# A two-layer trunk on one core: three plain items at the start of an up stage, residual rows scaled in the delta net's output projection, and five smaller edits beside them

## The chip, the cores and the metric

The kernel runs on one core of one Trainium2 chip. The metric is the device time of one execution in microseconds (us), the median of three runs. TensorE (PE in the profile) does the matrix products, VectorE (DVE) and ScalarE (ACT) the elementwise work, GpSimd (POOL) some of it, and SyncE (SP) issues most of the transfers between HBM and on-chip memory. Each engine works through its own instructions in a fixed order.

## The reference, cut to what matters

```python
e = jax.nn.silu(c @ cond_w + cond_b)
for i in range(2):                       # x is 1024 x 1024, f32
    sh1, sc1, g1, sh2, sc2, g2 = split(e @ ada_w[i] + ada_b[i], 6)
    y = mixers[i](x * (1 + sc1) + sh1)   # 0: gated delta net, 8 heads; 1: retention, 4 heads
    x = layer_norm(DN_ALPHA * x + (1 + g1) * y, ln_g[i, 0], ln_b[i, 0])
    y = conv_ffn(x * (1 + sc2) + sh2, ffn_up[i], ffn_conv_w[i], ffn_conv_b[i], ffn_down[i])
    x = layer_norm(DN_ALPHA * x + (1 + g2) * y, ln_g[i, 1], ln_b[i, 1])

def conv_ffn(h, w_up, conv_w, conv_b, w_down):      # hidden width 2816
    gate, up = split(h @ w_up, 2)
    gate = causal_dwconv(gate, conv_w) + conv_b     # 3 taps
    return (silu(gate) * up) @ w_down
```

The delta net projects h to q, k, v and a gate z, passes q, k and v through a causal convolution with 4 taps, solves one unit triangular system for every chunk of 64 positions, scans the chunks with a running state, and projects back. Retention projects to q, k, v and a gate, rotates q and k, and runs chunks of 128 positions with a running state.

## The kernel before, in words

Activations are kept transposed, as tiles of 128 features by 512 positions (a *half* is 512 of the 1024 positions). Nearly every product of two f32 matrices is made of three matmuls (`mm3`, lines 110 to 112, and line 637): each factor is split into a high part and a low rest, by one copy on ACT (line 89) and one subtraction on DVE (line 90). So before most matmuls stands a chain: a load by SP (`wr`), ACT, DVE, PE.

The stages follow one another: a short start that forms `e`; the delta net (`run` plans its order; on the profile's clock about 50 to 640 us); its output projection `proj_ln` in two halves (640 to about 770); up stage of the first feed-forward (about 750 to 1200); its down stage `proj_gen` (1200 to 1500); up stage of retention (about 1480 to 1780); retention's cores with `ret_fill` beside them (1780 to about 2150); output projection of retention; up stage (about 2290 to 2735) and down stage (to the end) of the second feed-forward.

**The delta net.** `run()` holds a clock of its own and takes the ready stream with the lowest number next; streams yield estimated times from the table `LAT`. `t_solve` (one call for four heads) does a forward substitution on DVE: 31 steps of two operations (lines 806 and 808), between a transpose into `Y` and two out, `RX` and `TX`. After every second step it yields `LAT["fs"]`, and other streams come in. `filler` is the stream of projection matmuls (tiles `acc<-hT,wl` and `acc<-hT,wh` in the views) that fill PE while DVE solves; each of its items also brings a convolution on DVE (line 456), a split, and at its end one `bg_step`. A `bg_step` does one unit of work left over from elsewhere: for `bg_ada` it is one load of 512 KB of `ada_w` (tile `mvw`) and two operations on DVE (lines 214 and 216), which form the modulation vectors of later stages as a matvec off PE. In this stage and in retention the load's tile has the tag `wr`, which the weight loads share; `bg_tag` names it.

**The up stages** are `strassen`. An *item* is a pair of weight blocks with a sink for its four outputs; two items, a gate and an up, make one of 11 pairs. All items but the first run as `wino`, which needs seven block products instead of eight, with DVE forming sums of weight blocks (`psub`, line 1205, `mm<-wr`) and of activations (`build_T`: tiles `T1` to `T4`). The first two items run plain, eight products each (tiles `acc<-hT,W`), while the activations are not ready: their first sides before `build_T` (kept in `ah`), the second sides behind it. `build_T` needs f32 values of the first half, which exist only as high and low parts, so PE adds the two with the identity (`joined`, line 402, `mm<-hT,ident_r`). `conv` (line 1579) is the gate's convolution. For retention (`direct`) the first sides go straight to their sinks; its sinks hold the rotations, and from item 8 on `scale_rows` has POOL multiply and add rows for the next residual (lines 1699 and 1700).

**The down stage** `proj_gen` reads its residual rows with `xload`; for the first half POOL scales them by `ln_g` and `ln_b` (line 1361). At the end of the kernel `norm` normalises the result's rows and stores them: the right half by ACT and POOL, the left by DVE (lines 1395 to 1403).

Of the kernel before, what the change touches and what calls it, by code (L numbers as in the profile page):

```python
# [11 lines left out]
AF = mybir.ActivationFunctionType  # L12
# [21 lines left out]
def trunk_kernel(ctx: ExitStack, tc, A):  # L34
# [82 lines left out]
    bg_tag = ["wr"]  # L117
# [83 lines left out]
    def bg_ada(i, j, kind):  # L201
        box = {}

        def unit(nh, kp):
# [3 lines left out]
            wr = tl(bg_tag[0], [P, 2, HALF], name="mvw")  # L208
            c0 = j * D + nh * HALF
            sp.dma_start(wr, A["ada_w"][i, kp * 256:(kp + 1) * 256, c0:c0 + HALF].rearrange("(a p) n -> p a n", p=P))  # L210
            for kk in range(2):
                k = kp * 2 + kk
                if k == 0:
                    dve.tensor_scalar(a, wr[:, 0], e[:, 0:1], None, ALU.mult)
                else:
                    dve.scalar_tensor_tensor(a, wr[:, kk], e[:, k:k + 1], a, ALU.mult, ALU.add)  # L216
# [157 lines left out]
    def ln_hooks(half, xts, tag, vecs2, out, dst, key, npool=0):  # L374
        def build(f):
            out.append(build_one(tag, xts, *vecs2(), f, pool if f < npool else dve))
        return ([lambda f=f: build(f) for f in range(KT)]
                + [lambda t=t: ln_store(half, t, xts, dst, key) for t in range(4)])

    def build_T(B, xts, scale, shift, tags, direct):  # L380
# [31 lines left out]
        def rest():  # L412
            if direct:
                for k in range(4):
                    t1, b22 = raw[k]
                    x11 = joined(B["11"][k])
                    dve.tensor_sub(b22, b22, t1)
                    put("T3", k, b22)
                    dve.tensor_add(b22, b22, x11)
                    put("T2", k, b22)  # L420
                    dve.tensor_sub(t1, t1, x11)
                    put("T1", k, t1)
                    dve.tensor_sub(b22, joined(B["21"][k]), b22)
                    put("T4", k, b22)
                return
            for k, (t1, b22) in enumerate(raw):
                dve.tensor_sub(t1, t1, joined(B["11"][k]))
                put("T1", k, t1)
            for k, (t1, b22) in enumerate(raw):
                dve.tensor_sub(b22, b22, t1)  # L430
                put("T2", k, b22)
            for k, (t1, b22) in enumerate(raw):
                dve.tensor_sub(t1, b22, joined(B["11"][k]))
                put("T3", k, t1)
            for k, (t1, b22) in enumerate(raw):
# [261 lines left out]
    def give(tag, n):  # L697
        free[tag] += n
# [88 lines left out]
    def t_solve(qd_):  # L787
        yield after_ev(("T0", 2 * qd_ - 1), ("A", 2 * qd_), ("A", 2 * qd_ + 1))
        yield from take("lane", 1)
        X = tl("lane", [P, 32, 32], name="X")  # L790
# [27 lines left out]
        give("lane", 1)  # L818
        emit(("Tq", qd_))
# [228 lines left out]

    def filler(items):
        spare = [(z, k) for k in range(GH)]  # L1050
        todo = list(items)
        while todo or spare:
# [39 lines left out]
            bg_step(acc_tile)  # L1092

    LAT = {"kk": 3.05, "ld": 1.14, "g1": 17.30, "gm": 2.50, "mm": 1.81, "T": 4.98, "X": 3.38, "fs": 1.9, "T0": 5.00, "t1": 1.65, "t2": 2.35, "t3": 1.34, "D": 2.67, "s1": 1.60, "s2": 1.22, "s3": 1.26, "tail": 12.31, "ssq": 9.30, "fv": 2.85}
# [58 lines left out]
    def strassen(hT0, xts, scale, shift, items, tags=("hTb", "hTb", "qkv", "qkv", "aux"), direct=False, beside=None, spare="lane"):  # L1153
# [19 lines left out]
        for n in range(2):  # L1173
# [6 lines left out]
            ahead.append([tl("cv", [P, 516], name="ah")[:, 0:HALF] for _ in range(2)])  # L1180
            for t, x in zip(ahead[n], X):
                act.activation(t, x, AF.Copy)
        rest = build_T(B, xts, scale, shift, tags, direct)
# [24 lines left out]
        def wino(n, sink):  # L1208
            ua, ub = items[n][:2]
            wa, wb = tl("wr", [P, D]), tl("wr", [P, D])  # L1210
            sp.dma_start(wa, ua)
            anchor["i"] = sp.dma_start(wb, ub)
            if beside:
                beside(n)
            a11, a12, a21, a22 = wa[:, hs(0)], wa[:, hs(1)], wb[:, hs(0)], wb[:, hs(1)]
# [26 lines left out]
        for n in range(2):  # L1242
# [11 lines left out]
        for n in range(2, len(items)):  # L1254
# [731 lines left out]
```

## Time and profile before

| | |
|---|---|
| median of the three runs | 2977.0 us (2974.75, 2977.0, 2977.12) |
| the profiled execution's own time | 2971.39 us |
| its span on the core | 2969.6 us |
| PE busy | 2819.0 us (95%) |
| DVE busy | 2214.7 us (75%) |
| ACT busy | 1323.3 us (45%) |
| POOL busy | 598.5 us (20%) |
| DMA, mean | 149 GB/s, 442.34 MB |

A time is read with its span: 1.8 us lie around the span. Busy shares are means over very unlike stages, so the views that matter are those of one stage or one stretch: the timeline of an engine with its idle times and what ended them, and the busy time by stretch.

### The profile page before, as it was taken

To read this page: it belongs to the slowest core of one execution; us is meant where nothing else is said; L and a number is where in the kernel's file an instruction comes from. 1 tells how busy PE (TensorE), PEld (TensorE's weight loads), DVE (VectorE), ACT (ScalarE), POOL (GpSimd) and SP (SyncE) were. 2 spreads that over 40 slices of the span, in tenths; PEclk is the share of its full clock that TensorE was granted. 3 is DMA by queue.
4 is the path that set the end of the run, shared out by engine and by line. 5 is a ranking of instruction groups with operands and counts; after the bars stand their busy time and mean duration, and the time that the engine had idled before them with its cause. 6 is when DMAs were issued, how large, how long until landed. Compare 5 with 4: busy or idle time off the path is not lost.

```text
span 2969.6 us, 38837 instructions
## 1 busy us (share of the span) xinstructions
PE 2819.0 (95%) x13654; PEld 2302.7 (78%) x13654; DVE 2214.7 (75%) x3863; ACT 1323.3 (45%) x2463; POOL 598.5 (20%) x625
## 2 busy tenths in 40 slices
PE   8889998999999999999999989999999899999997
PEld 7768877887778888777787777767778678888786
DVE  5795687546688888997677765666787787778889
ACT  4655555433444444536533332222345544445443
POOL 0411221134011111520002330322201011112603
PEclk9999999999999999999999999999999999999999
DMA  7222221344244444863424453556574243325753
GB/s 276 88 75 70 98 90 65 114 165 144 104 149 156 163 157 148 320 198 124 158 84 145 161 212 116 165 170 184 180 246 151 95 138 107 106 100 196 246 178 118
DMA packets 235378, 442.34 MB, mean 149 GB/s; under 512 B 22192, under 2 KB 75696, under 8 KB 235184
## 3 DMA queue, kind: packets, MB, share of 16 engines
q1 hardware_dynamic: 205024, 387.96, 38.7%
q10 hardware_dynamic: 25152, 34.61, 3.2%
q0 software_dynamic: 5008, 17.30, 1.5%
q8 instruction: 107, 1.75, 0.2%
q14 instruction: 87, 0.71, 0.1%
HBM read 331.26 MB, written 108.53 MB: 148 GB/s over the span
## 4 chain that ended last, share of the span: by engine, by line
PE 67%; DVE 15%; DMA 7%; issue 6%; ACT 3%; POOL 1%; SPq 0%; DVEq 0%; ACTq 0%; POOLq 0%
PE acc L637 15%; PE acc L1463 9%; PE acc L1159 8%; PE acc L110 5%; PE acc L111 5%; PE acc L112 5%; PE sc L1159 4%; PE sc L637 4%; PE sc L1463 2%; PE mm L637 2%; PE sc L110 2%; PE sc L111 2%; PE sc L112 2%; DMA mvw<-in_ada_w 1%; DVE qkv L456 1%
## 5 line engine op out<-in xcount | busy, mean ns | idle before, releaser
L1463 PE MATMUL acc<-bb,ab 128*128 128x512 f32 x1800 | 429.5, 393 | 5.3 <-DVE bb L90 3.6
L1463 PEld LDWEIGHTS acc<-bb,ab 128*128 128x128 f32 x1800 | 338.1, 189 | 79.9 <-DVE bb L90 5.9
L637 PE MATMUL acc<-hT,wh 128*128 128x512 f32 x960 | 301.1, 395 | 0.0
L1600 POOL TENSOR_TENSOR o<-o 128x512 f32<-128x512 f32 x88 | 118.4, 1356 | 725.3 <-DVE o L1593 690.3
L1159 PE MATMUL acc<-T,wb 128*128 128x512 f32 x840 | 204.8, 393 | 9.5 <-DVE wb L90 9.5
L637 PEld LDWEIGHTS acc<-hT,wh 128*128 128x128 f32 x960 | 183.3, 191 | 34.2
L637 PE MATMUL acc<-hT,wl 128*128 128x512 f32 x480 | 203.5, 424 | 0.2 <-ACT sg L1085 0.2
L89 ACT ACTIVATE ab<-ar 128x512 fp32r<-128x512 f32 x210 | 129.2, 624 | 149.7 <-PE acc L1463 75.0
L1159 PEld LDWEIGHTS acc<-T,wb 128*128 128x128 f32 x840 | 158.0, 189 | 46.6 <-DVE wb L90 13.8
L90 DVE TENSOR_TENSOR ab<-ar,ab 128x512 fp32r<-128x512 f32 x210 | 171.3, 822 | 28.3 <-ACT ab L89 28.0
L90 DVE TENSOR_TENSOR wb<-wr,wb 128x512 fp32r<-128x512 f32 x162 | 115.7, 719 | 88.7 <-ACT wb L89 86.8
L90 DVE TENSOR_TENSOR wl<-wr,wh 128x1024 fp32r<-128x1024 f32 x85 | 104.7, 1232 | 88.3 <-ACT wh L89 88.3
L89 ACT ACTIVATE wh<-wr 128x1024 fp32r<-128x1024 f32 x101 | 106.8, 1059 | 127.4 <-PE acc L637 62.2
L90 DVE TENSOR_TENSOR wb<-mm,wb 128x512 fp32r<-128x512 f32 x216 | 145.0, 684 | 20.4 <-ACT wb L89 18.5
L89 ACT ACTIVATE wb<-mm 128x512 fp32r<-128x512 f32 x216 | 122.4, 593 | 76.5 <-DVE mm L1205 76.2
L1218 ACT ACTIVATE pc<-acc 128x512 f32<-128x512 f32 x143 | 84.7, 592 | 158.6 <-PE acc L1159 106.5
L89 ACT ACTIVATE wb<-wr 128x512 fp32r<-128x512 f32 x162 | 99.2, 626 | 91.6 <-DMA wr<-in_ffn_up 48.8
L637 PE MATMUL acc<-wh,hT 128*128 128x512 f32 x384 | 136.9, 419 | 2.2 <-DVE vv L90 1.1
L1579 DVE SCALAR_TENSOR_TENSOR o<-g,vc,o 128x512 f32<-128x512 f32 (+2 forms) x176 | 135.1, 787 | 0.7
L456 DVE SCALAR_TENSOR_TENSOR qkv<-raw,vc,qkv 128x512 f32<-128x512 f32 x144 | 114.7, 800 | 28.0 <-ACT qkv L454 27.0
L110 PE MATMUL acc<-T,wb 128*128 128x512 f32 x292 | 116.4, 399 | 17.1 <-DVE wb L90 16.5
L216 DVE SCALAR_TENSOR_TENSOR ada<-mvw,e,ada 128x512 f32<-128x512 f32 x140 | 106.7, 762 | 25.1 <-DMA mvw<-in_ada_w 24.9
(636 smaller groups left out, 7056.8 us busy)
## 6 DMA issues: line engine op xcount, KB each, us to landing
wr<-in_ffn_up SPq DMA_DIRECT2D x96, 512.0 KB, 4.3
mvw<-in_ada_w SPq DMA_DIRECT2D x80, 512.0 KB, 4.2
ad<-o SPq DMA_DIRECT2D x154, 256.0 KB, 2.3
ar<-ad SPq DMA_DIRECT2D x154, 256.0 KB, 3.9
Br<-in_ffn_down SPq DMA_DIRECT2D x66, 256.0 KB, 3.7
wr<-in_ret_wv SPq DMA_DIRECT2D x32, 512.0 KB, 3.6
ar<-od SPq DMA_DIRECT2D x56, 256.0 KB, 4.8
xs<-xt ACTq DMA_DIRECT2D x24, 512.0 KB, 3.0
```

The source lines that it names most:

```text
L89: act.activation(dst_h, src, AF.Copy)
L90: eng.tensor_tensor(dst_l, src, dst_h, ALU.subtract)
L110: mm(acc, wl[:, k], hl[0], start=first, stop=False)
L111: mm(acc, wh[:, k], hl[1], start=False, stop=False)
L112: mm(acc, wh[:, k], hl[0], start=False, stop=last)
L216: dve.scalar_tensor_tensor(a, wr[:, kk], e[:, k:k + 1], a, ALU.mult, ALU.add)
L456: dve.scalar_tensor_tensor(oh, raw[:, 3 - j:515 - j], w[:, 3 - j:4 - j], oh, ALU.mult, ALU.add)
L637: pq(pe.matmul(out, lhsT, rhs, start=start, stop=stop, **kw), cost)
L1159: return pe.matmul(*a, skip_group_check=True, **kw)
L1463: mm_ = (lambda *a, p=p, onto=onto, **kw: (mm if p < 2 else pe.matmul)(*a, skip_group_check=onto, **kw))
L1579: dve.scalar_tensor_tensor(tv, gv[:, c0 - j:c1 - j], w[:, 2 - j:3 - j], tv, ALU.mult, ALU.add)
L1600: pool.tensor_tensor(o[d], o[x], o[y], op)
```

## The change

The edits, in the order of the program:

1. `bg_tag` is `"xT"` in the delta net and in retention: a load of `ada_w` goes, as two loads of 256 KB, into a ring of two tiles of its own; elsewhere it is as before.
2. `filler` counts the `bg_step` calls that it owes; while a `t_solve` runs it makes none, and behind it up to two per item. `LAT["fs"]` goes from 1.9 to 2.2.
3. The first half's rows of x behind the first layer norm are scaled by `ln_g` and `ln_b` on DVE before they are stored, in the hooks of `proj_ln`'s second half (`store_scaled`, 16 operations), and the down stage of the first feed-forward no longer scales them on POOL (16 fewer).
4. `build_T` has one order, that of retention, for all up stages: per k instead of per tile name, with 8 joins instead of 12.
5. The up stages of the feed-forwards run three items plain instead of two: 12 matmuls more in each (8 products of 12 instead of 7). The third item's first side waits in two `xT` tiles.
6. In retention's up stage every third raw weight block is loaded in two halves into `xT` tiles: a third buffer beside two of `wr`.
7. `scale_rows` comes with items 4 to 11 instead of 8 to 15.
8. `norm` at the end does both halves on DVE, with four operations of two steps.

```diff
-    bg_tag = ["wr"]
+    bg_tag = ["xT"]
...
+            if bg_tag[0] == "xT":
+                wr = [tl("xT", [P, HALF], name="mvw") for _ in range(2)]
+                for a2 in range(2):
+                    sp.dma_start(wr[a2], src[:, a2])
...
+    def store_scaled(t, xts, dst, key, grows):
+        for hf in range(2):
+            for r, op in zip(grows, (ALU.mult, ALU.add)):
+                dve.tensor_tensor(xts[t][:, hs(hf)], xts[t][:, hs(hf)], r[hf], op)
+        ln_store(0, t, xts, dst, key)
...
         def rest():
-            if direct:
-                for k in range(4):
...
-            for k, (t1, b22) in enumerate(raw):
-                dve.tensor_sub(t1, t1, joined(B["11"][k]))
-                put("T1", k, t1)
...
+            for k in range(4):
+                t1, b22 = raw[k]
+                x11 = joined(B["11"][k])
+                dve.tensor_sub(b22, b22, t1)
+                put("T3", k, b22)
+                dve.tensor_add(b22, b22, x11)
+                put("T2", k, b22)
+                dve.tensor_sub(t1, t1, x11)
+                put("T1", k, t1)
                 dve.tensor_sub(b22, joined(B["21"][k]), b22)
                 put("T4", k, b22)
...
     def t_solve(qd_):
...
+        busy.append(qd_)
...
+        busy.clear()
...
-            bg_step(acc_tile)
...
+            owed[0] += 1
+            for _ in range(0 if busy else min(owed[0], 2)):
+                bg_step(acc_tile)
+                owed[0] -= 1
...
-        for n in range(2):
+        nd = 2 if direct else 3
+        for n in range(nd):
             X = side(n, 0)
...
-            wa, wb = tl("wr", [P, D]), tl("wr", [P, D])
-            sp.dma_start(wa, ua)
-            anchor["i"] = sp.dma_start(wb, ub)
+            raws = []
+            for m, u in ((2 * n, ua), (2 * n + 1, ub)):
+                if direct and m % 3 == 0:
+                    raws += [tl("xT", [P, HALF], name="wr") for _ in range(2)]
+                    for h2 in range(2):
+                        anchor["i"] = sp.dma_start(raws[-2 + h2], u[:, hs(h2)])
...
-        for n in range(2, len(items)):
+        for n in range(nd, len(items)):
...
-            if half == 0 and gain:
+            if half == 0 and gain and not scaled:
                 for r, op in zip(grows, (ALU.mult, ALU.add)):
                     for hf in range(2):
                         pool.tensor_tensor(xt[:, hs(hf)], xt[:, hs(hf)], r[hf], op)
...
-                dve.tensor_tensor(mv[:, 6:7], mv[:, 2:3], mv[:, 3:4], ALU.mult)
-                act.activation(hi, hi, AF.Identity, bias=mv[:, 6:7], scale=mv[:, 3:4])
-                dve.scalar_tensor_tensor(lo, lo, mv[:, 2:3], gB[0], ALU.add, ALU.mult)
-                dve.scalar_tensor_tensor(lo, lo, mv[:, 3:4], bB[0], ALU.mult, ALU.add)
...
-                pool.tensor_tensor(hi, hi, gB[1], ALU.mult)
-                pool.tensor_tensor(hi, hi, bB[1], ALU.add)
+                for h2 in range(2):
+                    dve.scalar_tensor_tensor(xt[:, hs(h2)], xt[:, hs(h2)], mv[:, 2:3], gB[h2], ALU.add, ALU.mult)
+                for h2 in range(2):
+                    dve.scalar_tensor_tensor(xt[:, hs(h2)], xt[:, hs(h2)], mv[:, 3:4], bB[h2], ALU.mult, ALU.add)
...
-        for u in range(2 * (n - 8), 2 * (n - 8) + 2) if n >= 8 else ():
+        for u in range(2 * (n - 4), 2 * (n - 4) + 2) if 4 <= n < 12 else ():
...
+    bg_tag[0] = "xT"
     events["core", -1] = clk[0]
     free["qkv"] = 20
     run([(0.0, ret_fill())] + [(-1.0, core(h)) for h in range(RH)])
+    bg_tag[0] = "wr"
```

The compiler's scheduler reorders what the program issues, so the order of an engine says more than the diff. Three places follow. A row is a line of the kernel, an operation, the tile written and those read, and its shape; the lines are those of the kernel that the row belongs to (line 1579 before is line 1592 after, 1205 is 1212, 216 is 223, 954 is 955, 456 is 455).

The first place is DVE where the first feed-forward's up stage turns from plain items to `wino`. `T_...` are the tiles of `build_T`, the last of them from its last join, `mm<-wr` is a sum of weight blocks for the first product on `T1`, `o<-g` is the gate's convolution, and `wb<-mm,wb` is the split that releases the first matmul on `T1`. Before, directly below the three rows that use the last join:

```order
L1565 TENSOR_TENSOR g<-sc,pc 128x512
L1205 TENSOR_TENSOR mm<-mm,wr 128x512
L90 TENSOR_TENSOR T_7262<-bt,T_7261 128x512
L1579 SCALAR_TENSOR_TENSOR o<-g,vc,o 128x511
L1579 SCALAR_TENSOR_TENSOR o<-g,vc,o 128x512
L1579 SCALAR_TENSOR_TENSOR o<-g,vc,o 128x511
L214 TENSOR_SCALAR ada<-mvw,e 128x512
L1579 SCALAR_TENSOR_TENSOR o<-g,vc,o 128x512
L1579 SCALAR_TENSOR_TENSOR o<-g,vc,o 128x510
L1579 SCALAR_TENSOR_TENSOR o<-g,vc,o 128x511
L1579 SCALAR_TENSOR_TENSOR o<-g,vc,o 128x512
L90 TENSOR_TENSOR wb<-mm,wb 128x512
```

After, likewise directly below the rows that use the last join:

```order
L1605 TENSOR_TENSOR sc<-sc,pc 128x512
L1592 SCALAR_TENSOR_TENSOR o<-g,vc,o 128x511
L1592 SCALAR_TENSOR_TENSOR o<-g,vc,o 128x512
L1592 SCALAR_TENSOR_TENSOR o<-g,vc,o 128x511
L1592 SCALAR_TENSOR_TENSOR o<-g,vc,o 128x510
L1592 SCALAR_TENSOR_TENSOR o<-g,vc,o 128x512 x2
L1592 SCALAR_TENSOR_TENSOR o<-g,vc,o 128x511
L1592 SCALAR_TENSOR_TENSOR o<-g,vc,o 128x510
L1592 SCALAR_TENSOR_TENSOR o<-g,vc,o 128x512
L1592 SCALAR_TENSOR_TENSOR o<-g,vc,o 128x511
L1592 SCALAR_TENSOR_TENSOR o<-g,vc,o 128x512 x2
L90 TENSOR_TENSOR wb<-mm,wb 128x512
```

Between the use of the last join and the split for the first product on `T1` stand seven convolution operations and one of line 214 before, and twelve convolution operations after. On PE five matmuls stand between the last join and the first matmul on `T1` before, and eleven after. The place is the same at the start of the second feed-forward.

The second place is DVE at the end of the second `t_solve`: the last steps of the substitution (`fs`, `T`), the transposes (`RX`, `TX`) and the `DT<-DT,mm` for which PE waits. Before:

```order
L808 TENSOR_TENSOR T<-T,fs 128x4x28
L806 TENSOR_TENSOR fs<-Y,T 128x87
L808 TENSOR_TENSOR T<-T,fs 128x3x29
L806 TENSOR_TENSOR fs<-Y,T 128x60
L808 TENSOR_TENSOR T<-T,fs 128x2x30
L806 TENSOR_TENSOR fs<-Y,T 128x31
L808 TENSOR_TENSOR T<-T,fs 128x31
L812 STREAM_TRANSPOSE RX<-T 128x1024
L216 SCALAR_TENSOR_TENSOR ada<-mvw,e,ada 128x512
L816 STREAM_TRANSPOSE TX<-TP 128x1024
L954 TENSOR_TENSOR DT<-DT,mm 128x512 x3
```

After:

```order
L808 TENSOR_TENSOR T<-T,fs 128x2x30
L455 SCALAR_TENSOR_TENSOR qkv<-raw,vc,qkv 128x512
L920 TENSOR_TENSOR qkv<-mm,ir 128x512
L806 TENSOR_TENSOR fs<-Y,T 128x31
L90 TENSOR_TENSOR wl<-wr,wh 128x1024
L455 SCALAR_TENSOR_TENSOR qkv<-raw,vc,qkv 128x512
L808 TENSOR_TENSOR T<-T,fs 128x31
L955 TENSOR_TENSOR DT<-DT,mm 128x512
L812 STREAM_TRANSPOSE RX<-T 128x1024
L920 TENSOR_TENSOR qkv<-mm,ir 128x512
L816 STREAM_TRANSPOSE TX<-TP 128x1024
L955 TENSOR_TENSOR DT<-DT,mm 128x512 x3
```

The `ada` operations are gone from the solve, and filler work stands deeper in it. Counted from the transpose into `Y` to the one into `RX`, the first solve holds 18 convolution operations, 5 of `ada` and 3 splits `wl` before, and 24, 5 and 4 after; the second 22, 9 and 3 before, and 25, none and 4 after. On PE, 63 filler matmuls stand before and 108 after between the last `acc<-cst,qkv` ahead of the first solve's end and the products that wait for it; at the second solve 171 stand before and 213 after, from the last group of four `mm<-qkv` ahead of the wait. Behind the last operation of the scan 111 filler matmuls stand before and 57 after.

The third place is SP at the start of retention, with the loads of q and k (`qk`), of rows (`xlo`), of the weights for v (`wr<-in_ret_wv`) and of `ada_w`. Before:

```order
L1858 DMA qk<-qd 128x512 x2
L1717 DMA xlo<-xs_67 128x512 x2
L1858 DMA qk<-qd 128x512 x10
L102 DMA wr<-in_ret_wv 128x1024
L1717 DMA xlo<-xs_67 128x512 x2
L102 DMA wr<-in_ret_wv 128x1024
L1823 DMA gt<-gd 128x4x128
L1858 DMA qk<-qd 128x512 x4
L102 DMA wr<-in_ret_wv 128x1024 x9
```

After:

```order
L1730 DMA xlo<-xs_67 128x512 x2
L1871 DMA qk<-qd 128x512 x2
L213 DMA mvw<-in_ada_w 128x512
L1871 DMA qk<-qd 128x512 x7
L1730 DMA xlo<-xs_67 128x512 x2
L102 DMA wr<-in_ret_wv 128x1024
L1836 DMA gt<-gd 128x4x128
L1871 DMA qk<-qd 128x512 x3
L213 DMA mvw<-in_ada_w 128x512 x2
L102 DMA wr<-in_ret_wv 128x1024 x2
L213 DMA mvw<-in_ada_w 128x512 x2
L102 DMA wr<-in_ret_wv 128x1024
```

Ten of the 16 half loads of `ada_w` now stand here, among the loads for q, k and v; before, the first of its eight loads stands 48 rows below the last row shown.

64 lines of the change are left out of this document (28 added, 36 removed).

## The prediction

> **What bounds the kernel now.** I read the page first, then busy time by stretch of the program, then the idle times on PE's timeline, one by one. The columns of the stretches are the length, then busy us and instructions (x) of PE, PEld, DVE, ACT and POOL, the granted clock, the DMA share and GB/s.
>
> ```profile
> span 2969.6 us, 38837 instructions
> PE 2819.0 (95%) x13654; PEld 2302.7 (78%) x13654; DVE 2214.7 (75%) x3863; ACT 1323.3 (45%) x2463; POOL 598.5 (20%) x625
> 160.00:400.00 240.00, 215.88 (x1563) 183.30 (x1562) 173.84 (x442) 129.39 (x298) 48.62 (x76) 0.97 0.24 82
> 400.00:640.00 240.00, 222.87 (x1571) 190.63 (x1570) 157.19 (x357) 116.89 (x287) 33.79 (x55) 0.96 0.30 103
> 730.00:840.00 110.00, 98.04 (x433) 78.42 (x432) 76.67 (x119) 53.83 (x84) 14.55 (x10) 0.95 0.34 118
> 1200.00:1420.00 220.00, 212.39 (x934) 172.15 (x933) 191.40 (x295) 111.92 (x206) 66.87 (x48) 0.99 0.64 218
> 1500.00:1780.00 280.00, 265.79 (x1148) 216.13 (x1147) 200.81 (x297) 99.14 (x173) 69.25 (x66) 0.98 0.44 156
> 1760.00:1780.00 20.00, 16.31 (x64) 12.61 (x65) 8.29 (x12) 7.28 (x12) 2.31 (x4) 0.86 0.99 354
> 1940.00:1990.00 50.00, 43.46 (x191) 32.84 (x190) 29.58 (x51) 9.47 (x16) 18.07 (x25) 0.96 0.67 205
> ```
>
> PE is the bound: 150.6 us of the span are all that it does not work. So an edit is worth what it takes from PE's idle time, plus its change in matmuls. The delta net (first two stretches) holds 24.1 + 17.1 us of idle time, the start of the up stage 12.0, retention's up stage 14.2, and 1940 to 1990 another 6.5.
>
> The profiled run took 2971.39 us, 0.19% below the median of 2977.0. I work out the sum against the profiled run and set it off from the median.
>
> **The solves (edits 1 and 2).** PE's two longest waits of the delta net, what DVE did in the first solve and its `ada` work in the second (groups of a stretch: count, busy us and mean ns, idle time before), and the end of the first solve:
>
> ```profile
> 222.14 2.08 PE L637 MATMUL mm<-qkv 128*128 128x128 f32 x8 [11.07 <-DVE DT L954]
> 472.48 2.08 PE L637 MATMUL mm<-qkv 128*128 128x128 f32 x8 [8.95 <-DVE DT L954]
> L456 DVE SCALAR_TENSOR_TENSOR qkv<-raw,vc,qkv 128x512 f32<-128x512 f32 x18 | 13.4, 746 | 0.1
> L216 DVE SCALAR_TENSOR_TENSOR ada<-mvw,e,ada 128x512 f32<-128x512 f32 x6 | 4.5, 742 | 1.9 <-DMA mvw<-in_ada_w 1.9
> L90 DVE TENSOR_TENSOR wl<-wr,wh 128x1024 fp32r<-128x1024 f32 x3 | 3.7, 1218 | 0.0
> L216 DVE SCALAR_TENSOR_TENSOR ada<-mvw,e,ada 128x512 f32<-128x512 f32 x9 | 6.7, 746 | 1.1 <-DMA mvw<-in_ada_w 1.1
> 218.49 1.25 DVE L816 STREAM_TRANSPOSE TX<-TP 128x1024 f32<-128x1024 f32 x1 [0.75 <-ACT TP L814]
> 218.52 0.80 SPq L946 DMA_DIRECT2D DT<-Ld  x2
> 221.40 1.36 DVE L954 TENSOR_TENSOR DT<-DT,mm 128x512 f32<-128x512 f32 x2 [1.67 <-DMA DT<-Ld]
> ```
>
> PE runs out of filler while DVE ends the solve, with 2.9 us of transpose and `DT` load behind it. The order decides the size: first solve, 45 filler matmuls more ahead of the wait, at 0.227 us (pitch shown below) 10.2 us more cover; against it DVE gets six convolutions at 0.75 us and one split at 1.2, 5.7 us more. That leaves the stall 4.5 us shorter, and `ada` loads landing earlier can take off some of the 1.9 us; I take -5. Second solve: 42 matmuls more, 9.5 us, and on DVE 9 `ada` operations less (6.7 us and 1.1 of waits) against three convolutions and a split more (3.4 us): 13.9 us against a stall of 8.95. I take -8, since DVE's work there may in turn wait for PE, and -1.5 for the slow clock behind it (below). Together -14.5, between 0 (what is moved ahead is missed later) and -20.0 (both stalls gone). The cover was taken from behind the scan: 111 filler matmuls there become 57, 12.3 us less; I take 57 x 0.227 = 12.9 us to be enough. `ada` work put off goes to the scan's DVE time, busy 157.19 of 240 us, and two of its units to the first down stage.
>
> **The up-stage starts (edits 4 and 5), twice.** PE stops at the first product on `T1`, and DVE is why. Both engines there, and the same place in the second feed-forward:
>
> ```profile
> 811.03 0.39 PE L111 MATMUL sc<-hT,wb 128*128 128x512 f32 x1
> 811.26 0.39 PE L112 MATMUL sc<-hT,wb 128*128 128x512 f32 x1
> 819.91 0.80 PE L110 MATMUL acc<-T,wb 128*128 128x512 f32 x1 [8.26 <-DVE wb L90]
> 820.50 0.63 PE L111 MATMUL acc<-T,wb 128*128 128x512 f32 x1
> 820.93 0.63 PE L112 MATMUL acc<-T,wb 128*128 128x512 f32 x1
> 824.77 0.63 PE L112 MATMUL acc<-T,wb 128*128 128x512 f32 x1
> 826.15 3.03 PE L1159 MATMUL acc<-T,wb 128*128 128x512 f32 x12 [0.76 <-DVE wb L90]
> 2354.04 0.80 PE L110 MATMUL acc<-T,wb 128*128 128x512 f32 x1 [8.26 <-DVE wb L90]
> 809.84 1.39 DVE L436 TENSOR_TENSOR bt<-mm,bt 128x512 f32<-128x512 f32 x2 [3.16 <-PE mm L402]
> 814.14 2.07 DVE L1579 SCALAR_TENSOR_TENSOR o<-g,vc,o 128x511 f32<-128x511 f32 x3
> 816.52 2.73 DVE L1579 SCALAR_TENSOR_TENSOR o<-g,vc,o 128x512 f32<-128x512 f32 x4
> 819.17 0.68 DVE L90 TENSOR_TENSOR wb<-mm,wb 128x512 fp32r<-128x512 f32 x1
> ```
>
> Matmuls start 0.23 us apart at full clock and 0.43 behind the stall (820.50, 820.93), for 12 of them: 2.4 us. The title's edit puts 20 us more of plain matmuls ahead of this place, which would cover the wait, but the order moves the last join along with them. From the join on, DVE has 2 operations at 0.6 us and line 214 less, and five convolutions at 0.66 (2.07 for 3) more: +1.7 us; PE has six matmuls more between join and product, 1.4 us. So the stall stays, 8.6 us, and the slow clock with it. The wait of 0.76 us behind it stands after five convolutions and five multiplications more: 0 to +2, I take +1. Twelve matmuls for the third item less eight for joins: +0.9. Per start +2.2, together +4.4; the ends are -21.3 (both stalls and slow stretches gone) and +10.
>
> The slow stretch lasts 819.91 to about 825.2. The Trainium skill, "TensorE: Matmul & The Clock Gate", Part 1, says that an idle window of about 3.4 us halves the clock, and about as long a time of work restores it. The trace agrees on the halving; it shows 5.2 us to restore where the rule has 3.4, by which the stretch would cost 1.6 us instead of 2.4. A stall that shrinks but stays above that window gains nothing here by either.
>
> **POOL beside DVE (edits 3 and 8).** In the down stage, and at the end:
>
> ```profile
> 1286.07 6.47 POOL L1361 TENSOR_TENSOR xt<-xt,rowb 128x512 f32<-128x512 f32 x4 [12.54 <-DMA xt<-xs]
> 1286.20 1.77 DVE L1306 TENSOR_TENSOR Br<-Bw 128x512 f32<-128x512 f32 x1
> 1293.83 0.70 PE L1463 MATMUL sc<-bb,ab 128*128 128x512 f32 x2 [1.40 <-DVE ab L90]
> 2959.52 1.74 DVE L1445 TENSOR_TENSOR xt<-xt,pa 128x512 f32<-128x512 f32 x1
> ```
>
> Beside POOL a DVE operation takes 1.77 us instead of 0.68. Sixteen of these POOL operations go, so DVE gains 16 x 1.09 = 17.4 us and gets 16 `ada` operations (12 us). Of that PE gains what it waits there: 7.6 us idle from 1200 to 1420, one wait of 1.40 directly behind the slow row. I take -2 (0 to -5). By the Trainium skill, "SBUF — State Buffer", Who interferes with whom, an operation of DVE with two inputs on chip waits out the whole GpSimd instruction; that would free DVE by 16 x 1.62 = 25.9 us, and PE by no more than the 7.6. The 16 operations on DVE in the projection cost it 16 x 0.6 = 9.6 us; most lie beside PE's products, the first are queued ahead of the first half's last steps: +1 (0 to +9.6). The last rows have one slowed operation and a chain over three engines less: -2 (-4 to +1), their extra DVE work (12 x 0.6) lying mostly beside PE.
>
> **Retention (edits 1, 6 and 7).** In the up stage a weight load comes late and DVE with it; in the cores DVE waits for `ada_w`:
>
> ```profile
> 1704.24 1.15 ACT L89 ACTIVATE wb<-wr 128x512 fp32r<-128x512 f32 x2 [4.51 <-DMA wr<-in_ret_wg]
> 1704.90 1.29 DVE L90 TENSOR_TENSOR wb<-wr,wb 128x512 fp32r<-128x512 f32 x2 [2.29 <-ACT wb L89]
> 1719.25 4.61 PE L1159 MATMUL acc<-T,wb 128*128 128x512 f32 x12 [3.59 <-DVE wb L90]
> 1974.78 1.54 DVE L216 SCALAR_TENSOR_TENSOR ada<-mvw,e,ada 128x512 f32<-128x512 f32 x2 [5.20 <-DMA mvw<-in_ada_w]
> 1984.45 0.75 DVE L216 SCALAR_TENSOR_TENSOR ada<-mvw,e,ada 128x512 f32<-128x512 f32 x1 [5.02 <-DMA mvw<-in_ada_w]
> 1987.65 1.65 PE L637 MATMUL sc<-vv,sThl 128*128 128x512 f32 x3 [4.10 <-DVE Sr L1791]
> ```
>
> A third raw buffer ends the wait of 2.29 us, and the stall of 3.59 with its slow matmuls (4.61 us for 12, against 3.03 above) shrinks to about 1.3: -2.3 - 1.6, so -4 for the stage, and `scale_rows` only changes which items meet POOL. Bounds 0 and -14.2, the stage's whole idle time. With `ada` loaded earlier DVE's waits of 5.20 and 5.02 leave that place, and PE's 4.10 goes: -4 (0 to -6.5). At 1760 to 1780 the DMA engines are full (0.99); ten half loads, 2.6 MB, at 354 GB/s are 7.4 us there if they come in that stretch. They stand mostly behind the first loads, and some `qk` loads go earlier: -1 (-3 to +7.4).
>
> **Sum**: -14.5 + 4.4 - 2 + 1 - 2 - 4 - 4 - 1 = -22.1 us. Against the profiled run 2949.3; against the median 2977.0 - 22 = 2955.
>
> **Rivals.**
> 1. *The starts gain too*: another ready operation reaches DVE ahead of the convolutions, and the 20 us of plain work hide the chain. Against it: both engines work in order. -21.3 instead of +2.6 (beside the 1.8 of matmuls): 2955 - 23.9 = 2931. Chance 0.10.
> 2. *The delta net gives it back*: 57 filler matmuls do not cover the chain behind the scan, and the 12.3 us moved forward are missed at its end: 2955 + 12 = 2967. For it: PE's total work there is the same. Chance 0.15.
> 3. *The change does little*: DVE, not filler, still ends both solves, and 16 of the 22 us stay: about 2971 to 2977. Chance 0.07.
> 4. *Slower, by SP's queue at the start of retention*: the ring for `ada_w` has two tiles, so each new pair waits until DVE has read the one before, and the loads of weights for v behind it on SP wait too. Five pairs at 5.1 us (the waits at 1974 and 1984) are 26 us, and the 5 of retention are not gained: 2986. It decides above 4.6 us per pair. Against it: DVE is lightly used there (8.29 of 20 us). Chance 0.08.
>
> The forecast has 0.60. About 0.2% (6 us) is what a measurement of this kernel can tell from no change. Faster: 0.60 + 0.10 + most of rival 2 (0.13) = 0.83; same 0.09; slower 0.08. The range 2931 to 2976 takes in rivals 1 to 3.
>
> **What would show it.** Right: waits for `DT` of about 6 and under 2 us; a stall of 8 to 9 us at the first `T1` product of both up stages, behind twelve convolutions; no slowed DVE rows near 1286; no wait for `mvw` beyond 2 us in retention. Wrong: short stalls at the starts (rival 1), gaps of several us where the projection begins (2), waits for `DT` as long as before (3), or PE waiting for `wv` or `qk` near 1780 to 1830 (4).

## The result: slower by 1.8%

The changed kernel takes 3031.05 us (median of four runs, 3029.82 to 3033.32), the kernel before 2977.06: a ratio of 1.0181, 95% interval 1.0165 to 1.0197. The prediction was 2955 us, faster, so it was wrong in sign and by 76 us.

The profiled run took 3033.32 us with a span of 3031.5. The page's first lines:

```profile
span 3031.5 us, 38922 instructions
PE 2844.8 (94%) x13662; PEld 2325.9 (77%) x13662; DVE 2215.0 (73%) x3863; ACT 1325.8 (44%) x2455; POOL 560.9 (19%) x597
```

PE has 8 matmuls more (13662 against 13654 recorded) and is busy 25.8 us longer; it also waits 36.1 us longer. Where, a table of stages says; a stage's start is its first matmul on PE's timeline.

| stage (us) | before | after | difference | forecast |
|---|---|---|---|---|
| start, up to the delta net's first `gm` product | 107.9 | 111.8 | +3.9 | in the next |
| delta net | 546.8 | 538.3 | -8.6 | -14.5 |
| its output projection | 95.1 | 105.3 | +10.2 | +1 |
| first up stage | 459.6 | 514.3 | **+54.7** | +2.2 |
| first down stage | 226.4 | 228.6 | +2.2 | -2 |
| retention's up stage | 384.1 | 373.1 | -11.0 | -5 |
| retention's cores | 273.6 | 265.1 | -8.5 | -4 |
| retention's output projection | 190.4 | 190.4 | 0.0 | 0 |
| second up stage | 452.6 | 471.2 | **+18.6** | +2.2 |
| second down stage and end | 233.0 | 233.4 | +0.4 | -2 |

The two up stages cost 73.3 us, more than the whole loss of 62 between the spans; the rest gains 11.4. The busy time of the two stages, before (columns as in the prediction):

```profile
749.84:1209.45 459.61, 446.96 (x1962) 362.73 (x1961) 376.35 (x595) 221.14 (x417) 57.14 (x45) 0.99 0.45 153
2283.97:2736.61 452.64, 439.85 (x1933) 360.66 (x1932) 343.47 (x536) 220.91 (x379) 63.61 (x49) 0.99 0.35 121
```

and after:

```profile
755.36:1269.66 514.30, 462.41 (x1964) 376.32 (x1965) 388.16 (x589) 227.66 (x419) 61.10 (x45) 0.95 0.41 140
2326.90:2798.14 471.24, 448.54 (x1937) 366.77 (x1936) 344.04 (x527) 222.23 (x377) 64.08 (x49) 0.97 0.34 119
```

In the first, PE's idle time rose from 12.7 to 51.9 us, and its busy time by 15.5 us with only two recorded matmuls more: the granted clock fell from 0.99 to 0.95. PE's timeline after, over the whole program and in order of time, with the waits that answer to those shown of before, and new ones:

```profile
227.79 0.58 PE L636 MATMUL mm<-qkv 128*128 128x128 f32 x1 [5.54 <-DVE DT L955]
482.00 0.38 PE L636 MATMUL mm<-qkv 128*128 128x128 f32 x1 [2.55 <-DVE DT L955]
731.84 0.69 PE L327 MATMUL acc<-wh,hl 128*128 128x512 f32 x1 [3.33 <-DVE t L357]
846.95 0.79 PE L110 MATMUL acc<-T,wb 128*128 128x512 f32 x1 [9.47 <-DVE wb L90]
854.89 0.80 PE L1165 MATMUL acc<-T,wb 128*128 128x512 f32 x1 [2.83 <-DVE wb L90]
987.67 0.54 PE L110 MATMUL acc<-T,wb 128*128 128x512 f32 x1 [4.06 <-DVE wb L90]
988.00 0.63 PE L111 MATMUL acc<-T,wb 128*128 128x512 f32 x1
1032.17 0.65 PE L110 MATMUL sc<-T,wb 128*128 128x512 f32 x1 [4.09 <-DVE wb L90]
1254.45 0.80 PE L110 MATMUL acc<-T,wb 128*128 128x512 f32 x1 [4.07 <-DVE wb L90]
1280.40 0.79 PE L1475 MATMUL acc<-bb,ab 128*128 128x512 f32 x1 [6.03 <-DVE ab L90]
2471.12 0.79 PE L110 MATMUL sc<-T,wb 128*128 128x512 f32 x1 [4.29 <-DVE wb L90]
2516.04 0.50 PE L110 MATMUL acc<-T,wb 128*128 128x512 f32 x1 [3.34 <-DVE wb L90]
```

The waits for `DT` and the wait at the first `T1` product came out as forecast (about 6, about 2, 8 to 9). What the prediction does not have at all is a wait of about 4 us that comes back with every pair of the first up stage, 44.5 us apart (987.67 to 1032.17): nine of them from 898 to 1254 us, 36.5 us in sum, and two in the second. Each is followed by some eight matmuls at half pace; by their starts on PE's timeline that is 15.7 us more in the first stage. Waits and slow matmuls together are 52 of its 54.7 us; in the second stage the two waits (7.6 us) and their slow matmuls (4.2) are 11.8 of 18.6.

The regular distance made the cause readable. In the second feed-forward the waits end after two pairs, and there the background queue holds eight units of `ada_w`, four to a pair; in the first it holds 40 and lasts the whole stage. One such wait, on all three engines:

```profile
983.01 0.60 PE L233 MATMUL mm<-cst,ada 128*128 128x128 f32 x4
984.82 0.22 ACT L235 ACTIVATION_READ_ACCUMULATOR ada<-mm 128x1 f32 x1
985.07 0.16 DVE L237 SCALAR_TENSOR_TENSOR v<-cs,vc 128x4 f32<-128x4 f32 x1 [0.37 <-ACT ada L235]
985.15 0.69 DVE L1212 TENSOR_TENSOR mm<-mm,wr 128x512 f32<-128x512 f32 x1
985.87 0.60 ACT L89 ACTIVATE wb<-mm 128x512 fp32r<-128x512 f32 x1 [0.84 <-DVE mm L1212]
986.93 0.68 DVE L90 TENSOR_TENSOR wb<-mm,wb 128x512 fp32r<-128x512 f32 x1
```

After four units a group ends: PE transposes the sums (983.01), ACT reads them in eight operations (to 985.04), DVE makes the vector. Only then comes DVE's next sum of weight blocks, a split, and PE at 987.67. Four of the eleven groups (the first two of the first stage, both of the second) form rows instead: PE sums with ones (`mm<-ada,ones`, two matmuls), and one operation on DVE (line 246) reads the result, with nothing on ACT. They bring the wait too: 4.29, 3.74, 4.29 and 3.34 us.

Before, the same chain is as long, but other matmuls cover it:

```profile
936.84 0.60 PE L226 MATMUL mm<-cst,ada 128*128 128x128 f32 x4
941.44 0.50 PE L110 MATMUL acc<-T,wb 128*128 128x512 f32 x1
```

From the first transpose to the product on `T1` it is 4.60 us before and 4.66 us after (983.01 to 987.67). Before, 17 matmuls stand on PE between the two (17 to 19 at each of the eleven groups), and PE waits 0.1 us; after, the group stands last on PE ahead of the `T1` product, and none stands between.

The seven-product items make two steps of background work each, so four units fill one pair. Before, these items began with a gate item, and each group ended behind an up item. With three plain items they begin with an up item, and each group ends behind a gate item, whose convolution is on DVE too. That this is why the scheduler places the group so late on PE is argued, not shown.

### The profile page after: what moved, and what is told of

Read it like the earlier page. It is cut to its first block, busy times and chain, and to the rows that moved or that the text cites. A ratio compares the mean times of both kernels' runs of the same rounds, so it can differ in the third digit from the quotient of the medians.

```text
span 3031.5 us, 38922 instructions
## 1 busy us (share of the span) xinstructions
PE 2844.8 (94%) x13662; PEld 2325.9 (77%) x13662; DVE 2215.0 (73%) x3863; ACT 1325.8 (44%) x2455; POOL 560.9 (19%) x597
## 4 chain that ended last, share of the span: by engine, by line
PE 72%; DVE 14%; DMA 6%; ACT 3%; issue 3%; SPq 1%; POOL 0%; DVEq 0%; ACTq 0%; POOLq 0%
PE acc L636 14%; PE acc L1475 11%; PE acc L1165 9%; PE acc L110 5%; PE acc L111 5%; PE acc L112 5%; PE sc L1165 4%; PE sc L636 4%; PE sc L1475 2%; PE mm L636 2%; DMA mvw<-in_ada_w 2%; PE sc L110 2%; PE sc L111 2%; PE sc L112 2%; DVE o L1592 1%
## 5 line engine op out<-in xcount | busy, mean ns | idle before, releaser
L90 DVE TENSOR_TENSOR ab<-ar,ab 128x512 fp32r<-128x512 f32 x210 | 160.8, 770 | 46.2 <-ACT ab L89 45.8
L1165 PEld LDWEIGHTS acc<-T,wb 128*128 128x128 f32 x840 | 159.6, 191 | 44.5 <-DVE wb L90 11.1
L90 DVE TENSOR_TENSOR wl<-wr,wh 128x1024 fp32r<-128x1024 f32 x93 | 116.0, 1247 | 84.4 <-ACT wh L89 82.2
L89 ACT ACTIVATE wh<-wr 128x1024 fp32r<-128x1024 f32 x109 | 115.5, 1060 | 125.1 <-PE acc L636 58.4
L90 DVE TENSOR_TENSOR wb<-mm,wb 128x512 fp32r<-128x512 f32 x208 | 138.6, 684 | 27.8 <-ACT wb L89 26.4
L1592 DVE SCALAR_TENSOR_TENSOR o<-g,vc,o 128x512 f32<-128x512 f32 (+2 forms) x176 | 145.7, 851 | 6.3 <-ACT o L1587 4.4
```

The source lines that it names most:

```text
L89: act.activation(dst_h, src, AF.Copy)
L90: eng.tensor_tensor(dst_l, src, dst_h, ALU.subtract)
L1165: return pe.matmul(*a, skip_group_check=True, **kw)
L1592: dve.scalar_tensor_tensor(tv, gv[:, c0 - j:c1 - j], w[:, 2 - j:3 - j], tv, ALU.mult, ALU.add)
```

## The experiments

Every time below is a median; the ratio is that to the kernel before on the same chip, with its 95% interval.

| run | edit | us | ratio |
|---|---|---|---|
| x1_nd2 | changed kernel, two plain items | 2947.9 | 0.9918 (0.9894 to 0.9943) |
| x2_phase | changed kernel, background work two steps further | 2971.0 | 0.9991 (0.9979 to 1.0002) |
| y1_psum | changed kernel, transposes into another buffer | 2986.1 | 1.0029 (1.0013 to 1.0045) |
| x4_oldT | changed kernel, old order of `build_T` | 3033.5 | 1.0201 (1.0183 to 1.0219) |
| z1_only5 | kernel before, three plain items | 3060.3 | 1.0267 (1.0240 to 1.0294) |
| x3_noscale | changed kernel without edit 3 | 3028.9 | 1.0187 (1.0167 to 1.0207) |
| y2_nd2_noscale | x1_nd2 without edit 3 | 2947.2 | 0.9895 (0.9870 to 0.9919) |
| y3_gtag | x1_nd2, delta net's `ada_w` in the weight ring | 2961.9 | 0.9945 (0.9923 to 0.9966) |
| y4_gowe | x1_nd2 without edit 2 | 2968.6 | 0.9971 (0.9960 to 0.9983) |
| y5_rtag | x1_nd2, retention's `ada_w` in the weight ring | 2961.3 | 0.9944 (0.9926 to 0.9963) |
| y6_raw3 | x1_nd2 without the third raw buffer | 2966.4 | 0.9966 (0.9950 to 0.9983) |
| y7_scr | x1_nd2, `scale_rows` with items 8 to 15 | 2949.1 | 0.9900 (0.9884 to 0.9916) |

**Two plain items again.**

```diff
-        nd = 2 if direct else 3
+        nd = 2
```

> The changed kernel with two plain items in all up stages, as before (edit 5 undone, the new order of build_T kept). Theory A: the third plain item is the cause of both losses in the feed-forwards' up stages. Then these stages, 514.3 and 471.2 us in the changed kernel, come back to within 5 us of 459.6 and 452.6, and the time is 2956 to 2965 us. Theory B: the new order of build_T (edit 4) is the cause. Then the up stages stay some 10 us or more above before, the waits of over 4 us in every pair stay in the first one, and the time is above 2990 us.

The up stages took 458.3 and 449.6 us, and the time fell by 83 us, 8 more than theory A's range allows. A holds; theory B is out. The other seven edits together are worth 0.8%: 2947.9 us is 7 below the 2955 forecast for all eight. At the start of the first up stage, PE and DVE in this run:

```profile
816.93 0.50 PE L110 MATMUL acc<-T,wb 128*128 128x512 f32 x1 [4.69 <-DVE wb L90]
812.89 3.39 DVE L1592 SCALAR_TENSOR_TENSOR o<-g,vc,o 128x512 f32<-128x512 f32 x5
816.20 0.68 DVE L90 TENSOR_TENSOR wb<-mm,wb 128x512 fp32r<-128x512 f32 x1
```

With two items the same place has six convolution operations ahead of the split (these five and one more) and PE waits 4.69 us; in the changed kernel it has twelve and waits 9.47:

```profile
835.02 0.68 DVE L435 TENSOR_TENSOR bt<-mm,bt 128x512 f32<-128x512 f32 x1
838.27 8.02 DVE L1592 SCALAR_TENSOR_TENSOR o<-g,vc,o 128x511 f32<-128x511 f32 x12
846.22 0.68 DVE L90 TENSOR_TENSOR wb<-mm,wb 128x512 fp32r<-128x512 f32 x1
```

**The phase of the background work.**

```diff
             if items[n][3]:
                 items[n][3]()
+            if n == 2:
+                bg_step()
+                bg_step()
```

> The changed kernel with two steps of background work (bg_step) added in the third plain item, so that a group of four units of ada_w ends behind an up item again, as before, and not behind a gate item. Theory A1: the wait of 4.1 us in each pair comes from the end of such a group (four transposes, eight operations on ACT, one on DVE that waits for them), which the third plain item moved into the gate's convolution. Then the waits of 4 us from 898 to 1254 us and the two in the second feed-forward go, each with some 2 us of slow clock: nine to ten times 6 us, time 2972 to 2985 us. Theory A2: it comes from the seven-product items beginning with an up item at all, with the background work in any phase. Then the waits stay at 4 us and the time within 6 us of 3031.

Three plain items remain; only the point at which each group ends is moved back behind an up item. The time fell by 60 us, even more than expected, to that of the kernel before. The largest group of waits of the stretch behind its start, first after, then in this run (count, busy us, mean ns, idle time before and its releaser):

```profile
L110 PE MATMUL acc<-T,wb 128*128 128x512 f32 x96 | 42.2, 439 | 24.1 <-DVE wb L90 24.1
```

```profile
L110 PE MATMUL acc<-T,wb 128*128 128x512 f32 x98 | 38.6, 394 | 0.5
```

24.1 us of waits on this form become 0.5, and the mean matmul goes from 439 to 394 ns as the clock stays up. A2 is out. On PE 17 or 24 matmuls stand again between each group and the next `T1` product. The stage takes 465.3 us, still 5.7 more than before and 7.0 more than with two items: the matmuls of the third item and the wait of 9.46 us that stays at its start. So the third plain item does not pay even in the good phase: 2971.0 us is 23 above x1_nd2, of which the two up stages hold 7.0 and 8.4 and the first down stage 5.4.

**Which resource the group's end holds.**

```diff
             sink(1, Z, u2)
-            bg_step()
+            bg_step(acc_tile)
...
             sink(2, prod(a22, "T4"), u3)
-            bg_step()
+            bg_step(acc_tile)
```

> The changed kernel (three plain items) in which the background work of the up stages writes its four transposes into an accumulator's PSUM buffer (ring acc, four buffers) instead of one of the two mm buffers, which hold the sums of weight blocks. Theory P: the waits of 4.1 us per pair come from that ring: the transposes stand last on PE in the gate item, and the second sum of the next item must wait until ACT has read them. Then the waits go as in the run with the shifted phase, and the time is 2965 to 2985 us. Rival: ACT and DVE are simply held up in their order by the group's end, whatever buffer it uses. Then waits of 3 to 4 us stay, and the time is 3020 to 3036 us.

```profile
L110 PE MATMUL acc<-T,wb 128*128 128x512 f32 x96 | 37.5, 390 | 0.2 <-DVE wb L90 0.2
965.27 0.69 DVE L1212 TENSOR_TENSOR mm<-mm,wr 128x512 f32<-128x512 f32 x1
971.05 0.65 PE L233 MATMUL acc<-cst,ada 128*128 128x128 f32 x4 [1.26 <-DVE ada L223]
```

The phase is the changed kernel's, bad for it, and these waits are gone: 45 us less. DVE's second sum of weight blocks now comes ahead of the group's transposes (965.27 and 971.05) and no longer behind them, so the `mm` buffers do tie the sums to the group, as theory P says. But with the buffer the order on PE changed too: 12 or 24 matmuls stand between each group and the next `T1` product, where the changed kernel has none. The kernel before shares that buffer and has no wait, so the buffer alone does not make it; whether a group last on PE would, with a buffer of its own, no run shows. 2986 us is 1 above the range given, and 15 above x2_phase. PE's idle times in the stage show what is left: one of 3.36 us at the first pair, which ends 5.3 us ahead of the group's first matmul and so is not the rival's, and six of 1.1 to 2.2 us in which the group's matmuls wait for the `ada` sums on DVE.

**The order of `build_T`.**

```diff
-        rest = build_T(B, xts, scale, shift, tags)
+        rest = build_T(B, xts, scale, shift, tags, direct)
```

(with the old `rest` inside it, as the first diff shows it)

> The changed kernel with the feed-forwards' build_T in its order of before (all T1 first, then T2, T3, T4; 12 joins): edit 4 undone, three plain items kept. Theory C: the new order puts the last join right ahead of the first product on T1, so the third plain item cannot cover the chain. Then the two waits of 9.47 us fall below 4 us and the time by 10 to 18 us, to 3013 to 3021 us; the waits of 4 us per pair stay. Rival: the twelve convolution operations ahead of the split make the wait, whatever the order. Then the waits stay above 7 us and the time is 3028 to 3036 us.

The waits at the starts were 10.11 us instead of 9.47. Theory C falls: with three plain items the order of `build_T` hardly moves that wait, and the row of twelve convolutions, 8.02 us in this run too, is what fills it.

**Edit 5 alone.**

```diff
-        for n in range(2):
+        nd = 2 if direct else 3
+        for n in range(nd):
```

(also in the two other loops of `strassen`, with the third `ah` in `xT` tiles)

> The kernel before with edit 5 alone: three items plain in the feed-forwards' up stages, all else as before. If the loss of the change is this edit and it does not depend on the others, the up stages grow as they do in the changed kernel with the old order of build_T (459.6 to 514, 452.6 to 474 us), and the time is 3047 to 3058 us, 2.4 to 2.7% above before. If the other edits bring part of it (the background work put off in the delta net, two units of which are left over for the down stage), it is 3025 to 3045 us.

81 us alone (the kernel before took 2979.5 us on that chip) against 83 undone: its loss does not hang on the other edits. 3060 us is 2 above the first range; as a ratio, 2.7%, it lies within it. Its up stages took 517.7 and 472.0 us, with the waits of 4.1 us per pair in both traces.

**Edit 3 undone**, with three and with two plain items:

```diff
-            hooks = ln_hooks(0, xts, "hTa", lambda: (sc2, sh2), hT0, x_mid, ("mid", i), BAL["gh"], grows0)
+            hooks = ln_hooks(0, xts, "hTa", lambda: (sc2, sh2), hT0, x_mid, ("mid", i), BAL["gh"])
```

(also where `grows0` is made and where it is handed on)

> The changed kernel without edit 3: POOL scales the first half's residual rows in the first down stage again, and the output projection's hooks only store. If the 16 operations on DVE in the projection are what lengthened it, the projection falls from 105.3 to 95 to 98 us, the down stage grows by 0 to 3 us, and the time is 3021 to 3028 us. If the projection was lengthened by something else (the filler taken from behind the scan), it stays above 102 us and the time at 3029 to 3036 us.

> Two plain items everywhere (as in x1_nd2, 2947.9 us) and edit 3 undone as well. If the projection's loss and the down stage's gain add up as they did with three plain items, the projection falls from 103.7 to 95 to 97 us, the down stage grows by 1 to 3 us, and the time is 2940 to 2944 us. If the rows scaled by POOL cost the first down stage more here, the time stays at 2946 to 2950 us.

The projection fell from 105.3 to 96.0 us and from 103.7 to 96.0, and the down stage grew by 1.6 and 1.0. The whole time hardly shows it: -2.1 us and -0.7, 1 us above the first expectation's range and in the rival's of the second, inside the scatter of the runs, though the spans of the profiled runs differ by 6.3 and 5.0. So by the stages the edit costs some 7 us, and by the medians it is not told from nothing. Why the projection grows, DVE's timeline after shows:

```profile
724.78 3.39 DVE L384 TENSOR_TENSOR xt<-xt,rowb 128x512 f32<-128x512 f32 x2
728.69 1.28 DVE L384 TENSOR_TENSOR xt<-xt,rowb 128x512 f32<-128x512 f32 x2
731.10 0.68 DVE L357 TENSOR_TENSOR t<-acc,g 128x512 f32<-128x512 f32 x1
```

The scaling (line 384) stands ahead of the operation of line 357 that empties an accumulator, and PE waits 3.33 us for it (731.84 above); two of the scalings took 1.7 us each beside POOL. y2_nd2_noscale is the lowest of the versions run, but not told apart from x1_nd2.

**The delta net's two edits, each undone.** The loads back in the weight ring:

```diff
-    bg_tag = ["xT"]
+    bg_tag = ["wr"]
```

> x1_nd2 with the delta net's loads of ada_w back in the weight ring (edit 1 undone there; retention keeps its own ring, the deferral of edit 2 stays). Theory G: the ring of its own lets the operations on ada_w come before the first convolutions and so costs the 3.9 us by which the delta net's start was later; the gain at the solves comes from the deferral. Then the start is at 107 to 109 us again, the delta net takes 534 to 540 us, and the time is 2942 to 2947 us. Rival: the ring of its own is part of the gain at the solves. Then the delta net takes 541 us or more and the time is 2950 us or more.

and the deferral undone:

```diff
-            owed[0] += 1
-            for _ in range(0 if busy else min(owed[0], 2)):
-                bg_step(acc_tile)
-                owed[0] -= 1
+            bg_step(acc_tile)
```

(with `"fs": 1.9`)

> x1_nd2 without edit 2: no deferral of background work during a solve, and 1.9 in the table again. Theory G: the waits for DT, 5.6 and 2.7 us with the deferral, go back to 8 us or more each, the delta net takes 543 to 549 us instead of 535.9, and the time is 2955 to 2962 us. Rival: the planner's new order matters little and the ring of its own gives the gain. Then the waits stay under 7 and 4 us, and the time is 2945 to 2951 us.

The ring undone, the delta net takes 544.0 us; the deferral undone, 554.4; neither undone, 535.9; both, as in the kernel before, 546.8. The ten profiled runs with both edits lie between 534.1 and 538.3, the two with neither both at 546.8. The two waits, without the ring and then without the deferral:

```profile
228.33 0.58 PE L636 MATMUL mm<-qkv 128*128 128x128 f32 x1 [5.86 <-DVE DT L955]
486.68 0.58 PE L636 MATMUL mm<-qkv 128*128 128x128 f32 x1 [5.27 <-DVE DT L955]
```

```profile
223.98 0.58 PE L636 MATMUL mm<-qkv 128*128 128x128 f32 x1 [11.08 <-DVE DT L955]
486.80 0.58 PE L636 MATMUL mm<-qkv 128*128 128x128 f32 x1 [19.05 <-DVE DT L955]
```

The deferral does the work, as theory G says, and more than it says, since stage and time lie 5 and 7 us above its ranges: a ring of its own without it makes the second wait worse than it was. The two halves of edit 2, the deferral and the number in the table, were not run apart. But the ring is a part of the gain, as y3's rival says: it is worth 8 us beside the deferral, and costs some 2 us at the start (109.3 instead of 111.8), less than the 3.9 expected; the other runs with the ring and the deferral have 110.2 to 111.8 there, the two with neither 107.9 and 109.4.

**Retention's edits, each undone.**

```diff
-    bg_tag[0] = "xT"
     events["core", -1] = clk[0]
```

> x1_nd2 with retention's loads of ada_w back in the weight ring (edit 1 undone in retention alone). Theory R: the 9 us by which retention's cores became shorter (273.6 to 264.4 us) come from these loads, for which DVE waited 5.2 and 5.0 us. Then the cores take 271 to 275 us again and the time is 2953 to 2959 us. Rival: they come from the loads for q and k standing earlier on SP, with the up stage's end. Then the cores stay at 263 to 267 us and the time at 2945 to 2951 us.

```diff
-                if direct and m % 3 == 0:
+                if False:
```

> x1_nd2 with two raw weight buffers in retention's up stage instead of three (edit 6 undone, scale_rows still with items 4 to 11). Theory W: the third buffer gave the 10 us of this stage (from its first product on T1 to the cores 324.9 before, 314.7 now). Then the stretch takes 320 to 325 us and the time is 2953 to 2959 us. Rival: moving scale_rows gave them. Then the stretch stays under 318 us and the time at 2946 to 2951 us.

```diff
-        for u in range(2 * (n - 4), 2 * (n - 4) + 2) if 4 <= n < 12 else ():
+        for u in range(2 * (n - 8), 2 * (n - 8) + 2) if n >= 8 else ():
```

> x1_nd2 with scale_rows back at items 8 to 15 (edit 7 undone, third buffer kept). Theory W, as above: the stretch stays within 2 us of 314.7, since POOL meets as many DVE operations in other items, and the time at 2945 to 2951 us. Rival: the move gave the gain; then the stretch takes 320 us or more and the time is 2953 us or more.

Each gain belongs to one edit. Without the ring in retention the cores take 273.3 us instead of 264.4, and a wait of 4.15 us for `Sr` is back; z1_only5, also without the ring, took 270.6, so the gain is between 4 and 10 us. Without the third raw buffer the stretch takes 324.6 us instead of 314.7; its first wait there, without and with:

```profile
1518.36 0.50 PE L1165 MATMUL sc<-T,wb 128*128 128x512 f32 x1 [3.59 <-DVE wb L90]
```

```profile
1516.27 0.50 PE L1165 MATMUL sc<-T,wb 128*128 128x512 f32 x1 [0.60 <-DVE wb L90]
```

`scale_rows` moved or not, it takes 312.6 or 314.7 us: nothing. The medians of y5_rtag and y6_raw3 miss their ranges by 2 and 7 us; they lie 7 to 8 us above the profiled runs (2953.6 and 2959.7), from which the stages are read, so it is the stages that carry these verdicts.

Edit 8 has no run of its own. The last stage took 230.8 to 236.3 us in the twelve profiled runs with it, 233.0 and 238.0 in the two without: its worth stays open.

## Why the prediction was wrong

- **The up-stage starts: the term that failed.** It was +2.2 us for each start and measured +54.7 and +18.6. At the start itself the two stalls held: the one forecast at 8.6 us behind twelve convolutions is 9.47, and the second one, 0.76 to at most 2.8, is 2.83. Yet by x2_phase, which has the start without the later waits, the two up stages are 5.7 and 5.3 us longer than before, not 2.2. The step that failed is the silent one, worth the other 49 and 13 us: that an edit of the start ends at the start. The third plain item changes which item of a pair every later group of background work ends behind, and that was looked at nowhere but at the two starts. The order after shows it at every pair that still has background work: the group's matmuls stand last on PE ahead of a `T1` product.
- **Rivals.** None of the four names this. The slower one, SP's queue at retention's start, had the right sign and is wrong: that stretch got faster.
- **The delta net.** Waits of about 6 and under 2 were forecast; 5.54 and 2.55 came. The stage gained 8.6 us (8.5 to 12.7 over all profiled runs) and not 14.5, and its start lost 3.9 that the sum lacks. New and longer waits took part of it: 2.78 us at the projection's first product, 2.59 us at 532 (1.39 before, at 537), and 4.14 us at 406, where 2.67 us stood at 397 before. Rival 2 is in this, at a quarter of its price.
- **POOL and DVE.** -2 us in the first down stage: -1.6 with two plain items; in the changed kernel +2.2, with a wait of 6.03 us at 1280 behind the last group of background work. It ends with one split on DVE that took 4.54 us (0.68 undisturbed) beside POOL's scaling of the other half's rows (line 1369), which edit 3 leaves where it was. The projection's +1 was mis-sized: +8 to +9 by undoing it, near the upper bound of 9.6, since the scalings stand ahead of the operation that empties an accumulator. The -2 for the last rows (edit 8) no run shows.
- **Retention.** The mechanisms are right, the sizes were half: -11.0 for -5, -8.5 for -4. The third buffer takes the waits of nearly all items, not of the one that was priced: PE's idle time from the first `T1` product to the cores is 17.2 us without it (y6_raw3) and 8.4 with it. DVE's longest wait for `mvw` is 2.64 us (at 1850.8), a little over the 2 us forecast and without a wait of PE; before it was 5.20.
- **The chances.** 0.83 for faster rested on single places, each priced well or badly, and on no look at the steady state of the longest stage. That the other seven edits come to 2947.9 us, near the 2955, is partly luck, as errors cancel (x1_nd2 against before): -7.1 us for start and delta net where -14.5 was forecast, +8.6 for the projection where +1 was, -19.5 for retention where -9 was.

## What to carry to other kernels

A change at the start of a loop shifts everything that runs beside the loop in a period of its own: find the item behind which the periodic work ends, before and after, and count that place times the loop's length. Where work is squeezed into another engine's gaps, look at which shared buffer it holds and for how long, not only at its busy time. Try the parts of a bundle one by one: here seven of the eight edits together gained 0.8%, and one lost 2.7 to 2.8%.

## What the runs showed of the hardware

Short waits were dear because of the clock. Rows of the changed kernel behind the waits of 4.06 us (987.67) and 3.34 us (2516.04):

```profile
990.56 0.63 PE L111 MATMUL acc<-T,wb 128*128 128x512 f32 x1
990.99 0.59 PE L112 MATMUL acc<-T,wb 128*128 128x512 f32 x1
991.41 0.40 PE L110 MATMUL acc<-T,wb 128*128 128x512 f32 x1
2516.61 0.39 PE L112 MATMUL acc<-T,wb 128*128 128x512 f32 x1
2516.84 0.40 PE L110 MATMUL acc<-T,wb 128*128 128x512 f32 x1
2517.84 0.63 PE L110 MATMUL acc<-T,wb 128*128 128x512 f32 x1
2518.27 0.63 PE L111 MATMUL acc<-T,wb 128*128 128x512 f32 x1
```

Behind the first, matmuls start 0.43 us apart from 988.00 to about 991.4, which is eight matmuls and 1.6 us more for a wait of 4 us. Behind the second they run at full pace (0.23 us apart) for about 1 us and only then at 0.43, so the clock did not fall at the wait's end. The Trainium skill, "TensorE: Matmul & The Clock Gate", Part 1, tells of a window of about 3.4 us that runs free of what the program does. The trace agrees. Stretches of the changed kernel behind the wait of 3.34 us, and one of the kernel before around the end of the wait of 8.26 us (columns as in the prediction, the granted clock third from the end):

```profile
2516.04:2517.16 1.12, 1.12 (x5) 0.94 (x6) 0.67 (x1) 0.42 (x1) 0.00 (x0) 1.00 0.00 0
2517.16:2520.57 3.41, 3.41 (x10) 2.64 (x9) 1.90 (x3) 0.67 (x2) 0.00 (x0) 0.50 0.04 11
815.41:825.65 10.24, 5.49 (x12) 3.81 (x12) 10.24 (x18) 4.94 (x9) 0.08 (x1) 0.50 0.07 26
```

The clock is at half for 3.41 us, or for three times that, and not from the wait's end on but from a point of its own: 1.1 us behind the wait of 3.34 us, and 4.5 us ahead of the end of the wait of 8.26 us. So the 5.2 us of slow matmuls that the prediction set against the rule are what was left of 10.24 us when the wait ended. A wait shorter than 3.4 us can cost the clock too: behind 2.55 us (482.00) it was at half for 3.41 us, behind 2.75 us (2136.47) it stayed full. So a bound of 3.4 us, as the prediction took it, is not safe.
